# Second product of an MLP: instructions of VectorE, GpSimd and ScalarE's casts tied to the order of the source

## The chip, the cores and the metric

The kernel runs on one core of a Trainium2 chip. A core has TensorE (PE: matmuls, with its weight loads shown apart as PEld), VectorE (DVE), ScalarE (ACT), GpSimd (POOL) and SyncE (SP, which here issues most DMAs). Each engine works through its own queue in the order in which the instructions stand there; engines wait for each other by semaphores. The metric is the time of one execution on the device in microseconds, the median of several runs.

## The reference

A block with two parallel mixers (a long convolution and gated linear attention), then a two-layer MLP. The change concerns only the end:

```python
def _sq_relu_mlp(h, w1, w2):
    return jnp.square(jax.nn.relu(h @ w1)) @ w2
...
        x = x + g2 * _sq_relu_mlp(h2, w_mlp1[l], w_mlp2[l])
...
    return _rms_norm(x, norm_final)
```

Here x has 2048 rows of 1024 and the MLP's inner width is 4096; all is float32. `g2` is a gate of 1024 columns.

## The kernel before

**Precision.** A float32 operand is split into a high part (a cast on ACT, `uh`, `wh`, `bh`) and a low part (a subtraction on DVE or POOL, `ul`, `wl`, `bl`), and a product is made of three matmuls: high by high, high by low, low by high.

**Seven products.** Both products of the MLP use a scheme of Strassen's kind: a 2 x 2 block product with seven multiplications m = 1 to 7 in the order 1, 2, 6, 5, 7, 4, 3 instead of eight. Sums of blocks are formed first (`sum_b`, L1243 and L1245, and the two subtractions L1464 and L1465 for a chunk of the second weights).

**The second product** is the loop over `at` from 0 to 63, called a step here: `t = at % 8` is a pair of row tiles and `g = at // 8` a part of the inner dimension. A step has seven *groups*, one for each m; a group is six matmuls of 128 x 128 by 512 (`full2`, L1640), three for each of two weights (`wh`/`wl` for kb = 0, `bh`/`bl` for kb = 1). Groups 4 and 3 of a step run late, within the next step (`late4`, `late3`), so in time a step runs 1, 2, 4 of the step before, 6, 3 of the step before, 5, 7. Three accumulators in PSUM serve a step; groups 1, 6, 7 and 4 go on in the same one, `x`, and after each group `more` (L1645) adds it to the rows in SBUF, `acc`, on DVE. So the addition after group 1 must be done before group 6 starts, and so on.

After a group, `refill` splits for the step after (for 4 and 3: for the group that is still to run): an operand `ur` into `uh` (L1598, ACT) and `ul` (L1599, POOL; DVE in step 0), and, where the weight changes, `w2_split`: `wh`/`bh` by ACT and `wl`/`bl` by DVE (the helper `split`, L231 and L232, before), with `sum_b` on DVE. `uh` and `ul` of each m have two buffers (odd and even steps), each weight one.

A **chunk** of the second weights is a tile `raw` of 128 x 5 x 512, loaded by SP (L1458), in one of two buffers. `w2_raw` returns six pieces of work: four *gates* (products with `g2b`, L1461, on POOL) and L1464 and L1465 (on DVE). The loop asks for a chunk in every fourth step (`at % 4 == 3`) and puts the six pieces into a list, `prep`, from which `slot()` takes one entry. `slot()` is called after each group's refill, seven times in a step, here numbered 0 to 6. By the source the gates of a chunk asked for in step 7 come in slots 1, 3 and 5 of step 8 and slot 0 of step 9, L1464 in slot 4 and L1465 in slot 6 of step 9, and its splits from step 10 on.

In the last eight steps a finished pair of row tiles is normalised: ACT squares it (L1660), POOL makes the factor (L1664, L279, L280: `ss`, `mrs`), and `finish` (L1669) scales it on DVE and stores it.

**What sets the order.** The source only traces instructions. A scheduler then orders each engine's queue by priority and by when it takes the inputs of an instruction to be ready; so an instruction may stand far ahead of its place in the source. `tc.keep_in_program_order(ins)` records, for one instruction, that it must come behind the instruction traced before it on its engine. It adds an order within the queue and no semaphore. It was used at one place so far, L323.

Of the kernel before, what the change touches and what calls it, by code (L numbers as in the profile page):

```python
# [10 lines left out]
F32 = mybir.dt.float32  # L11
# [3 lines left out]
ALU = mybir.AluOpType  # L15
# [195 lines left out]
def hybrid_block(ctx: ExitStack, tc, a, out, dbg=None):  # L211
    nc = tc.nc
# [5 lines left out]
    dve = nc.vector  # L218
    gps = nc.gpsimd
# [10 lines left out]
    def split(hi, lo, src):  # L230
        nc.scalar.copy(hi, src)  # L231
        dve.tensor_sub(lo, src, hi.bitcast(F32))  # L232

    dr = ctx.enter_context(tc.tile_pool(name="dram", bufs=1, space=DRAM))
    d_s = dr.tile([32, 128, DH], F32, name="d_s")
# [19 lines left out]
    def sb(name, side="left", stack=ctx):  # L255
        return stack.enter_context(tc.tile_pool(name=name, bufs=1, side=side, reuse_waits="tile"))
# [35 lines left out]
    def load_w(src):  # L292

        n = src.shape[-1]
        hi, lo = (wp.tile([P, KD * 264], F32R, tag=t, bufs=2, name=t)[:, 0:KD * n].rearrange("p (k n) -> p k n", k=KD)
                  for t in ("whi", "wlo"))
        for h in range(2):
            raw = wp.tile([P, 4 * 272], F32, tag="raw", bufs=1, name="raw")
            rk = raw[:, 0:4 * n].rearrange("p (k n) -> p k n", k=4)
            ks = slice(4 * h, 4 * h + 4)  # L300
            dma(rk, src[:, ks, :])
            split(hi[:, ks, :], lo[:, ks, :], rk)
        return hi, lo
# [706 lines left out]
    def load_wo(k):  # L1010
        raw = rawp.tile([P, D], F32, tag="raw", bufs=2, name="raw")
        dma(raw[:], a["w_out"][k * P:(k + 1) * P, :])
        split(woh[k // 4][:, k % 4, :], wol[k // 4][:, k % 4, :], raw[:])
# [3 lines left out]
    def load_y(t, a_):  # L1017
        yt = yop.tile([P, 4, P], F32, tag=f"yt{a_}", bufs=2, name="yt")
        dma(yt[:], d_yt[a_ * DH:(a_ + 1) * DH, t * P:(t + 1) * P].rearrange("(k p) t -> p k t", p=P))
        yh = yop.tile([P, 4, P], F32R, tag=f"yh{a_}", bufs=2, name="yh")  # L1020
        yl = yop.tile([P, 4, P], F32R, tag=f"yl{a_}", bufs=2, name="yl")
        split(yh[:], yl[:], yt[:])
        ys[t, a_] = (yh, yl)
# [197 lines left out]
    def raw_tile():  # L1221
        pool = rp[nraw[0] % len(rp)]
        nraw[0] += 1
        return pool.tile([P, 5, 512], F32, tag="raw", bufs=1, name="raw")
# [5 lines left out]
    PLACE = (0, 1, 2, 3, 4, 0, 1)  # L1230
# [9 lines left out]
    def sum_b(r, m, eng):  # L1240

        if m == 1:
            eng.tensor_sub(r[:, 0, :], r[:, 2, :], r[:, 4, :])  # L1243
        elif m == 2:
            eng.tensor_sub(r[:, 1, :], r[:, 1, :], r[:, 0, :])  # L1245

    def part(kp, h, j):
        return bp[kp].tile([P, 512], F32R, tag=f"b{h}{kp}_{j}", bufs=1, name=f"b{h}")
# [120 lines left out]
    g2b = sb("gp", stack=em).tile([P, D], F32, name="g2b")  # L1369
# [85 lines left out]
    def w2_raw(n, engs, eng=dve):  # L1455

        r = w2r[n] = raw_tile()
        dma(r[:, 0:4, :], a["w2"][n])  # L1458

        def gate(q):  # L1460
            engs[q].tensor_mul(r[:, q, :], r[:, q, :], g2b[:, (q // 2) * 512:(q // 2 + 1) * 512])  # L1461

        return [*(lambda q=q: gate(q) for q in range(4)),
                lambda: eng.tensor_sub(r[:, 4, :], r[:, 3, :], r[:, 0, :]),  # L1464
                lambda: eng.tensor_sub(r[:, 3, :], r[:, 2, :], r[:, 3, :])]  # L1465

    def w2_split(n, m):
        r, j, k = w2r[n], PR[m][1], PR[m][0]
        if n % 2:

            hi, lo = (part(0, h, j) for h in "hl")
        else:
            hi, lo = (wm.tile([P, 512], F32R, tag=f"w{h}{k}", bufs=1, name=f"w{h}") for h in "hl")
        split(hi[:], lo[:], r[:, PLACE[j], :])
        sum_b(r, m, dve)
        w2s[m, n % 2] = (hi, lo)

# [2 lines left out]
    for tb in range(2):  # L1480
# [8 lines left out]
        for at in range(1, 16):  # L1489
            n = ns[at]  # L1490
            w, nxt = wops, {}
            x, y = pt(), pt()
            r, rn = rw[n], None
            first = lambda m: w2_split(0, m) if tb and at == 15 else None
            if at < 15:
                rn = rw[ns[at + 1]] = w_raw(ns[at + 1])
            elif tb == 0:
                raws.append(fill_raw(1, 0, gps))
            else:
                for step in w2_raw(0, [gps] * 4):  # L1500
                    step()
# [21 lines left out]
            if at == 15 and tb == 0:  # L1523
                raws.append(fill_raw(1, 1, gps))
            elif at == 15:
                more_w2 = w2_raw(1, [dve] * 4)
# [47 lines left out]
    def row(at, m, kb):  # L1574
        return 2 * ((at + 8 - CHANGE[m, kb]) // 8 % 8) + kb
# [14 lines left out]
    def u_tile(at, h, m):  # L1590
        return uu[(h, m) not in U0 or at % 2].tile([P, 2, P], F32R, tag=f"u{h}{m}{at % 2}", bufs=1, name=f"u{h}")
# [3 lines left out]
    def split_u(at, m):  # L1595
        hi, lo = (first_u.pop((h, m)) if at == 0 and (h, m) in first_u else u_tile(at, h, m) for h in "hl")
        src = uts[at][:, :, ORDER.index(m), :]
        nc.scalar.copy(hi[:], src)  # L1598
        (gps if at else dve).tensor_sub(lo[:], src, hi[:].bitcast(F32))  # L1599
        ops[at, m] = (hi, lo)  # L1600

    load_u(0)
# [10 lines left out]
    def acc(t, i, j):  # L1613
        return acc4[t // 2][:, 2 * (t % 2) + i, j * 512:(j + 1) * 512]
# [3 lines left out]
    for m in (1, 2, 6):  # L1618
        w2_split(1, m)
        split_u(0, m)  # L1620
    for m in (5, 7):
        w2_split(1, m)
# [9 lines left out]
    for m in (5, 7):  # L1632
        split_u(0, m)
# [8 lines left out]

    def more(ps, t, i, j):

        dve.tensor_add(acc(t, i, j), acc(t, i, j), ps[:])  # L1645

    def refill(at, m):

        if at < NU:
            split_u(at, m)  # L1650
            for kb in range(2):
                n = row(at, m, kb)
                if n != row(at - 1, m, kb) if at else m in (4, 3):
                    w2_split(n, m)
# [7 lines left out]
    def scale_of(t, i):  # L1662
        ss = sums.pop((t, i))
        gps.tensor_add(ss[:, 2:3], ss[:, 0:1], ss[:, 1:2])  # L1664
        return rstd_of(mf, ss[:, 2:3], 1, 1.0 / D, "mrs")

    def finish(t, i, j, rs):
        v, tile = acc(t, i, j), 2 * t + i
        dve.scalar_tensor_tensor(v, v, rs[:], nf[:, j * 512:(j + 1) * 512], op0=ALU.mult, op1=ALU.mult)  # L1669
        dma(out[tile * P:(tile + 1) * P, j * 512:(j + 1) * 512], v)  # L1670

    def slot():
# [9 lines left out]
    for at in range(NU):  # L1682
        g, t = divmod(at, 8)
        prep, coming = prep + coming, []
        x, y = pt(), pt()
        full2(x, at, 1, True)
        more(x, t, 0, 0)
        refill(at + 1, 1)
        slot()
        z = pt()  # L1690
        full2(z, at, 2, True)
        more(z, t, 0, 0)
        refill(at + 1, 2)
        slot()
# [3 lines left out]
        slot()  # L1698
        full2(x, at, 6, False)
        more(x, t, 0, 1)  # L1700
        refill(at + 1, 6)
        slot()
# [8 lines left out]
        if at == 0:  # L1711
            coming = w2_raw(row(4, 1, 1), [gps] * 4, gps)
        elif at % 4 == 3 and at < 60:

            q = w2_raw(row(at + 5, 1, at // 4 % 2), [gps] * 4)
            coming = [v for step in q[:4] for v in (None, step)] + [None] * 3 + [q[4], None, q[5]]
        if at == 40:
            nf = mf.tile([P, D], F32, name="nf")
            dma(nf[:], a["norm_final"].partition_broadcast(P))
        if g == 7 and t:  # L1720
            for i, j in ((0, 0), (0, 1), (1, 0), (1, 1)):
                square(t - 1, i, j)
            for i in range(2):
                rs = scale_of(t - 1, i)
                ends.extend(lambda i=i, j=j, rs=rs, t=t: finish(t - 1, i, j, rs) for j in range(2))
# [28 lines left out]
    for i, rs in ((1, r1), (0, r0)):  # L1754
        for j in range(2):
            finish(7, i, j, rs)
# [18 lines left out]
```

## Time and profile before

| | |
|---|---|
| median of 3 runs | 2677.9 us (2675.67 to 2682.8) |
| profiled execution | 2688.92 us, span 2687.1 us |
| mean granted clock of TensorE | 0.959 |
| busy: PE, PEld, DVE, ACT, POOL | 93%, 77%, 60%, 44%, 40% |
| first matmul of the second product, last one | 1969.9 us, 2677.4 us |
| matmuls L1640 in it | 6 x 448 |

The profile shows one execution; its times are in microseconds from the first instruction. Rows of groups give a line of the kernel, the engine, the instruction and what it writes and reads, with buffer numbers left out. Idle time of an engine is put down to what came last of that for which it waited. The clock that TensorE is granted is a share of full speed.

### The profile page before, as it was taken

What the parts mean: (1) busy time and instruction counts of PE and PEld (TensorE: products, weight loads), DVE (VectorE), ACT (ScalarE), POOL (GpSimd) and SP (SyncE); (2) the same over time, 40 slices, a digit from 0 to 9 for tenths busy, and PEclk for the clock granted to TensorE, in tenths of its full rate; (3) what the DMA queues carried; (4) which work ended last, traced back from release to release, by engine and by line L of the source; (5) the groups of instructions that cost most, each with busy time, mean ns of one, the idle gap of its engine ahead of it and who ended that gap; (6) DMA issues with size and microseconds to landing.
All of it is one profiled execution on the core that took longest, in us unless ns stands there. A gap on an engine that the chain in (4) does not pass through costs nothing. (4 is left out here: it accounts for less than half of the span.)

```text
span 2687.1 us, 38017 instructions
## 1 busy us (share of the span) xinstructions
PE 2506.9 (93%) x13320; PEld 2076.7 (77%) x13320; DVE 1612.6 (60%) x2619; ACT 1185.2 (44%) x2273; POOL 1077.9 (40%) x1093
## 2 busy tenths in 40 slices
PE   9799999999998798899989998999978999999987
PEld 5678978897887787788778887888867777777776
DVE  5754366735567677744465557555556656666668
ACT  6464352225225555334455555555543333333334
POOL 2130231214112213142344443544466666666565
PEclk9899999999998798899999999999998999999999
DMA  5425444432548787556544545545483233323333
GB/s 194 140 86 175 123 134 141 140 117 92 174 148 197 200 238 202 185 169 210 162 144 142 165 137 169 169 141 165 135 310 124 99 114 112 114 99 114 112 125 129
DMA packets 304480, 406.09 MB, mean 151 GB/s; under 512 B 25108, under 2 KB 226712, under 8 KB 293920
## 3 DMA queue, kind: packets, MB, share of 16 engines
q1 hardware_dynamic: 301408, 395.27, 47.0%
q10 hardware_dynamic: 2880, 8.39, 0.8%
q8 instruction: 105, 1.72, 0.3%
q14 instruction: 87, 0.71, 0.1%
HBM read 273.49 MB, written 130.09 MB: 150 GB/s over the span
## 5 line engine op out<-in xcount | busy, mean ns | idle before, releaser
L1599 POOL TENSOR_TENSOR ul<-ur,uh 128x256 fp32r<-128x256 f32 x441 | 360.3, 825 | 209.5 <-ACT uh L1598 209.2
L1645 DVE TENSOR_TENSOR acc<-acc,ps 128x512 f32<-128x512 f32 x448 | 304.0, 683 | 156.8 <-PE ps L1640 154.1
L1598 ACT CAST uh<-ur 128x256 fp32r<-128x256 f32 x448 | 179.1, 406 | 410.3 <-PE ps L1640 378.4
L1384 PE MATMUL ps<-bh,wh 128*128 128x512 f32 x896 | 350.3, 393 | 5.0 <-ACT u L1392 2.1
L1384 PE MATMUL ps<-bl,wh 128*128 128x512 f32 x896 | 351.0, 392 | 4.0 <-DVE bl L232 4.0
L1384 PE MATMUL ps<-bh,wl 128*128 128x512 f32 x896 | 350.1, 391 | 4.1 <-DVE wl L232 4.1
L232 DVE TENSOR_TENSOR wl<-raw,wh 128x512 fp32r<-128x512 f32 x276 | 266.4, 977 | 98.0 <-ACT wh L231 95.4
L231 ACT CAST wh<-raw 128x512 fp32r<-128x512 f32 x276 | 170.6, 622 | 203.7 <-PE ps L1384 166.2
L1640 PE MATMUL ps<-wh,uh 128*128 128x512 f32 x448 | 185.1, 413 | 66.4 <-DVE acc L1645 59.2
L1384 PEld LDWEIGHTS ps<-bh,wh 128*128 128x128 f32 x896 | 169.5, 189 | 42.0 <-ACT tt L1350 3.3
L1384 PEld LDWEIGHTS ps<-bl,wh 128*128 128x128 f32 x896 | 169.5, 189 | 40.4 <-DVE bl L232 5.3
L1384 PEld LDWEIGHTS ps<-bh,wl 128*128 128x128 f32 x896 | 169.3, 189 | 40.4 <-DVE wl L232 5.3
L1640 PE MATMUL ps<-bl,uh 128*128 128x512 f32 x448 | 180.2, 402 | 0.0
L1640 PE MATMUL ps<-bh,ul 128*128 128x512 f32 x448 | 180.0, 402 | 0.0
L1640 PE MATMUL ps<-wl,uh 128*128 128x512 f32 x448 | 179.9, 401 | 0.0
L1640 PE MATMUL ps<-bh,uh 128*128 128x512 f32 x448 | 179.9, 401 | 0.0
L1640 PE MATMUL ps<-wh,ul 128*128 128x512 f32 x448 | 179.6, 401 | 0.0
L1640 PEld LDWEIGHTS ps<-wh,uh 128*128 128x128 f32 x448 | 88.6, 198 | 96.4 <-DVE acc L1645 63.4
L226 PE MATMUL ph<-hth,whi 128*128 128x512 f32 x384 | 150.9, 393 | 0.0
L228 PE MATMUL ph<-hth,wlo 128*128 128x512 f32 x384 | 149.6, 390 | 0.0
L227 PE MATMUL ph<-htl,whi 128*128 128x512 f32 x384 | 149.4, 389 | 0.0
L226 PE MATMUL pv<-whi,hth 128*128 128x264 f32 x512 | 146.7, 287 | 2.8 <-ACT whi L231 2.7
(291 smaller groups left out, 5727.4 us busy)
## 6 DMA issues: line engine op xcount, KB each, us to landing
raw<-in_w_dram SPq DMA_DIRECT2D x49, 1024.0 KB, 5.5
ur<-d_m SPq DMA_DIRECT2D x112, 448.0 KB, 3.9
d_m<-c SPq DMA_DIRECT2D x128, 256.0 KB, 2.6
d_m<-s SPq DMA_DIRECT2D x96, 256.0 KB, 3.4
xt<-in_x_dram SPq DMA_DIRECT2D x32, 512.0 KB, 4.8
mwt<-in_wada_dram SPq DMA_DIRECT2D x64, 256.0 KB, 3.0
raw<-in_wi_vg_dram SPq DMA_DIRECT2D x20, 528.0 KB, 4.8
wada<-in_wada_dram SPq DMA_DIRECT2D x16, 512.0 KB, 7.2
```

Source lines behind the costliest of these rows:

```text
L226: mm(ps, lh, rh, start=first, stop=False)
L227: mm(ps, lh, rl, start=False, stop=False)
L228: mm(ps, ll, rh, start=False, stop=last)
L231: nc.scalar.copy(hi, src)
L232: dve.tensor_sub(lo, src, hi.bitcast(F32))
L1384: mm(ps[:], x_[:, sl], y_[j], start=start and i == 0, stop=stop and i == 2, skip_group_check=True)
L1598: nc.scalar.copy(hi[:], src)
L1599: (gps if at else dve).tensor_sub(lo[:], src, hi[:].bitcast(F32))
L1640: mm(ps[:], x_[:, kb, :], y_[:], start=start and kb + i == 0, stop=kb == 1 and i == 2, skip_group_check=True)
L1645: dve.tensor_add(acc(t, i, j), acc(t, i, j), ps[:])
```

## The change

`pin` is the context's `keep_in_program_order`. It is put around the instructions of the second product on DVE and POOL (gates, L1464 and L1465, low parts, the additions after groups, the final scaling) and around the casts of ACT. `w2_split` no longer calls `split` but writes out the same two instructions. The matmuls, the DMAs, ACT's squares, `sum_b` and POOL's factors aren't pinned.

```diff
+    pin = tc.keep_in_program_order
...
         def gate(q):
-            engs[q].tensor_mul(r[:, q, :], r[:, q, :], g2b[:, (q // 2) * 512:(q // 2 + 1) * 512])
+            pin(engs[q].tensor_mul(r[:, q, :], r[:, q, :], g2b[:, (q // 2) * 512:(q // 2 + 1) * 512]))
 
         return [*(lambda q=q: gate(q) for q in range(4)),
-                lambda: eng.tensor_sub(r[:, 4, :], r[:, 3, :], r[:, 0, :]),
-                lambda: eng.tensor_sub(r[:, 3, :], r[:, 2, :], r[:, 3, :])]
+                lambda: pin(eng.tensor_sub(r[:, 4, :], r[:, 3, :], r[:, 0, :])),
+                lambda: pin(eng.tensor_sub(r[:, 3, :], r[:, 2, :], r[:, 3, :]))]
...
-        split(hi[:], lo[:], r[:, PLACE[j], :])
+        pin(nc.scalar.copy(hi[:], r[:, PLACE[j], :]))
+        pin(dve.tensor_sub(lo[:], r[:, PLACE[j], :], hi[:].bitcast(F32)))
         sum_b(r, m, dve)
...
-        nc.scalar.copy(hi[:], src)
-        (gps if at else dve).tensor_sub(lo[:], src, hi[:].bitcast(F32))
+        pin(nc.scalar.copy(hi[:], src))
+        pin((gps if at else dve).tensor_sub(lo[:], src, hi[:].bitcast(F32)))
...
-        dve.tensor_add(acc(t, i, j), acc(t, i, j), ps[:])
+        pin(dve.tensor_add(acc(t, i, j), acc(t, i, j), ps[:]))
...
-        dve.scalar_tensor_tensor(v, v, rs[:], nf[:, j * 512:(j + 1) * 512], op0=ALU.mult, op1=ALU.mult)
+        pin(dve.scalar_tensor_tensor(v, v, rs[:], nf[:, j * 512:(j + 1) * 512], op0=ALU.mult, op1=ALU.mult))
```

The new lines shift the numbers: in the changed kernel the gates are L1464, L1464 and L1465 are L1467 and L1468, L1599 is L1603, L1598 is L1602, L1645 is L1649, and the split of a weight is L1477 and L1478. Three places in the queues follow.

DVE before, around L1464 of the chunk `raw_18264`; the rows of `acc_17801` belong to steps 4 and 5 (`ps_18019` is `x` of step 5 and `ps_18020` its `y`), those of `acc_17990` to step 6:

```order
L1645 TENSOR_TENSOR acc_17801<-acc_17801,ps_18033 128x512
L1645 TENSOR_TENSOR acc_17801<-acc_17801,ps_17922 128x512
L1645 TENSOR_TENSOR acc_17801<-acc_17801,ps_18019 128x512
L1645 TENSOR_TENSOR acc_17801<-acc_17801,ps_17923 128x512
L1464 TENSOR_TENSOR raw_18264<-raw_18264 128x512
L1645 TENSOR_TENSOR acc_17801<-acc_17801,ps_18020 128x512
L1465 TENSOR_TENSOR raw_18264<-raw_18264 128x512
L1645 TENSOR_TENSOR acc_17801<-acc_17801,ps_18019 128x512
L232 TENSOR_TENSOR wl_18120<-raw_17890,wh_18119 128x512
```

DVE of the change, around the same subtraction of the same chunk (`ps_18391` and `ps_18392` are `x` and `y` of step 9, `acc_17609` stands for step 10):

```order
L1649 TENSOR_TENSOR acc_17481<-acc_17481,ps_18391 128x512
L1649 TENSOR_TENSOR acc_17481<-acc_17481,ps_18297 128x512
L1467 TENSOR_TENSOR raw_18264<-raw_18264 128x512
L1649 TENSOR_TENSOR acc_17481<-acc_17481,ps_18392 128x512
L1649 TENSOR_TENSOR acc_17481<-acc_17481,ps_18391 128x512
L1468 TENSOR_TENSOR raw_18264<-raw_18264 128x512
L1649 TENSOR_TENSOR acc_17609<-acc_17609,ps_18477 128x512
L1478 TENSOR_TENSOR bl_18491<-raw_18264,bh_18490 128x512
L1246 TENSOR_TENSOR raw_18264<-raw_18264 128x512
```

The subtraction moved from step 5 to step 9, the place of the source, right ahead of the splits that need it.

POOL before, around the four gates of that chunk; `ur_17992` holds the operands of step 7, `ur_17887` those of step 6 and `ur_18080` those of step 8:

```order
L1599 TENSOR_TENSOR ul_18149<-ur_17887,uh_18148 128x256
L1461 TENSOR_TENSOR raw_18264<-raw_18264,g2b_12328 128x512
L1599 TENSOR_TENSOR ul_18160<-ur_17992,uh_18159 128x256
L1461 TENSOR_TENSOR raw_18264<-raw_18264,g2b_12328 128x512 x3
L1599 TENSOR_TENSOR ul_18175<-ur_17887,uh_18174 128x256
L1599 TENSOR_TENSOR ul_18189<-ur_17992,uh_18188 128x256
```

POOL of the change, around the same four gates (`ur_18178` holds step 9, `ur_18261` step 10):

```order
L1603 TENSOR_TENSOR ul_18318<-ur_18178,uh_18317 128x256
L1464 TENSOR_TENSOR raw_18264<-raw_18264,g2b_12328 128x512
L1603 TENSOR_TENSOR ul_18330<-ur_18080,uh_18329 128x256
L1603 TENSOR_TENSOR ul_18345<-ur_18178,uh_18344 128x256
L1464 TENSOR_TENSOR raw_18264<-raw_18264,g2b_12328 128x512
L1603 TENSOR_TENSOR ul_18357<-ur_18080,uh_18356 128x256
L1603 TENSOR_TENSOR ul_18376<-ur_18178,uh_18375 128x256
L1464 TENSOR_TENSOR raw_18264<-raw_18264,g2b_12328 128x512
L1603 TENSOR_TENSOR ul_18388<-ur_18178,uh_18387 128x256
L1603 TENSOR_TENSOR ul_18401<-ur_18261,uh_18400 128x256
L1464 TENSOR_TENSOR raw_18264<-raw_18264,g2b_12328 128x512
```

The gates moved from the low parts for step 7 to those for steps 9 and 10, about two steps later, and stand one by one between them.

ACT before, at the first change of weights, in step 2 (`raw_17615` is the first chunk of the loop; `ur_17611` holds step 3, `ur_17703` step 4):

```order
L1598 CAST uh_17813<-ur_17611 128x256
L1598 CAST uh_17824<-ur_17611 128x256
L1598 CAST uh_17837<-ur_17703 128x256
L231 CAST bh_17742<-raw_17615 128x512
L1598 CAST uh_17849<-ur_17703 128x256
L231 CAST bh_17759<-raw_17615 128x512
```

ACT of the change, around the same two casts:

```order
L1602 CAST uh_17725<-ur_17514 128x256
L1602 CAST uh_17738<-ur_17611 128x256
L1477 CAST bh_17742<-raw_17615 128x512
L1602 CAST uh_17755<-ur_17611 128x256
L1477 CAST bh_17759<-raw_17615 128x512
```

The weight's first cast stood behind the first operand of step 4 and now stands behind the first operand of step 3.

## The prediction

> **What bounds the kernel now.** I read the share of busy time first, then the waits of the second product (from 1969.9 us on), then one of its stalls on all four engines, and last the windows of that stage. From the page and from the waits between 2000 us and the end (engine and line that waited, what it waited for: us in total, times, longest):
>
> ```profile
> span 2687.1 us, 38017 instructions
> DVE raw L1464 <- POOL raw L1461: 75.0, 15, 9.2
> PEld ps L1640 <- DVE acc L1645: 63.4, 24, 7.2
> PE ps L1640 <- DVE acc L1645: 59.2, 25, 6.8
> POOL raw L1461 <- DMA raw<-in_w_dram: 14.8, 13, 3.6
> ```
>
> TensorE (PE) waits for the additions L1645 on VectorE (DVE), and DVE waits 15 times, 5.0 us each, for GpSimd's (POOL's) gate products L1461. The weight loads (PEld) wait over the same gaps as the matmuls, so the two middle rows aren't added. One of the 15 in the timeline (start, duration, engine, instruction; in brackets the idle time before it and what ended it), DVE, POOL and PE apart:
>
> ```profile
> 2168.19 0.69 DVE L1645 TENSOR_TENSOR acc<-acc,ps 128x512 f32<-128x512 f32 x1 [0.67 <-PE ps L1640]
> 2173.93 1.20 DVE L1464 TENSOR_TENSOR raw<-raw 128x512 f32<-128x512 f32 x1 [5.05 <-POOL raw L1461]
> 2175.05 0.68 DVE L1645 TENSOR_TENSOR acc<-acc,ps 128x512 f32<-128x512 f32 x1
> ...
> 2167.46 1.29 POOL L1461 TENSOR_TENSOR raw<-raw,g2b 128x512 f32<-128x512 f32 x1 [0.94 <-DMA raw<-in_w_dram]
> 2168.71 0.74 POOL L1599 TENSOR_TENSOR ul<-ur,uh 128x256 fp32r<-128x256 f32 x1
> 2169.41 2.55 POOL L1461 TENSOR_TENSOR raw<-raw,g2b 128x512 f32<-128x512 f32 x2
> 2172.60 1.30 POOL L1461 TENSOR_TENSOR raw<-raw,g2b 128x512 f32<-128x512 f32 x1
> ...
> 2173.21 0.39 PE L1640 MATMUL ps<-bh,ul 128*128 128x512 f32 x1
> 2176.98 0.80 PE L1640 MATMUL ps<-wh,uh 128*128 128x512 f32 x1 [3.39 <-DVE acc L1645]
> 2177.58 0.63 PE L1640 MATMUL ps<-wl,uh 128*128 128x512 f32 x1
> 2181.84 0.63 PE L1640 MATMUL ps<-bh,ul 128*128 128x512 f32 x1
> ```
>
> DVE has nothing else to blame: it stands at L1464 from 2168.9 to 2173.9 while POOL multiplies four rows, the first of them held by its load. The additions behind L1464 come late, PE runs dry, and its next matmuls start 0.426 us apart ((2181.84 - 2177.58) / 10 between the eleven in these rows). In a stretch without a stall they start 0.2266 us apart, 20.17 us for 89 intervals:
>
> ```profile
> 2144.65 0.39 PE L1640 MATMUL ps<-bh,ul 128*128 128x512 f32 x1
> ...
> 2164.82 0.39 PE L1640 MATMUL ps<-bl,uh 128*128 128x512 f32 x1
> ```
>
> The windows of the stage, cut at the restarts of PE (us; busy time and count of PE, PEld, DVE, ACT, POOL; granted clock, DMA share, GB/s):
>
> ```profile
> 1969.88:2020.00 50.12, 38.69 (x151) 30.58 (x151) 25.92 (x38) 14.79 (x42) 41.44 (x45) 0.87 0.83 311
> 2019.94:2048.60 28.66, 26.05 (x102) 20.97 (x102) 15.88 (x24) 9.59 (x22) 17.63 (x22) 0.90 0.39 130
> 2048.61:2565.11 516.50, 480.82 (x2016) 392.10 (x2016) 318.72 (x469) 181.12 (x420) 329.78 (x385) 0.95 0.33 110
> 2565.12:2609.50 44.38, 39.88 (x168) 32.54 (x168) 26.50 (x40) 18.05 (x45) 28.72 (x37) 0.96 0.36 121
> 2609.51:2678.00 68.49, 62.16 (x252) 47.45 (x252) 60.86 (x85) 31.63 (x86) 43.85 (x68) 0.98 0.36 128
> ```
>
> At 0.2266 us a matmul these stretches would take 34.2, 23.1, 456.8, 38.1 and 57.1 us. So they lose **15.9, 5.5, 59.7, 6.3 and 11.4 us**, 98.8 together. The third one holds twelve periods of four steps (168 matmuls), each 5.0 us too long.
>
> **What the change moves.** It adds and removes no arithmetic: the same multiplications, casts and subtractions, in another order. In the order before, L1464 of a chunk of weights stood four steps ahead of its place in the source (for the chunk raw_18264 in step 5, not 9), and its gates in one block among the low parts for step 7. Now the gates stand singly between the low parts that steps 8 and 9 issue, the last in slot 0 of step 9, and L1464 in slot 4 of step 9. Between the last gate and L1464 lie four more slots, that is four groups of six matmuls, 4 x 6 x 0.2266 = 5.4 us. POOL needs 1.29 us for the gate, so L1464 finds it done.
>
> *Term 1, the periodic stalls: 5.5 + 59.7 + 6.3 = 71.5 us.* All of it goes if nothing else is late. What is late next, by engine, in one step of 7 groups, 9.52 us:
> DVE: seven additions at 0.60 (their spacing when queued: 2175.05 to 2175.65 below), and where weights are split up to three subtractions and two sums at 0.60, each subtraction behind its cast (0.65):
>
> ```profile
> 2175.65 0.68 DVE L1465 TENSOR_TENSOR raw<-raw 128x512 f32<-128x512 f32 x1
> 2150.49 0.69 DVE L232 TENSOR_TENSOR wl<-raw,wh 128x512 fp32r<-128x512 f32 x1 [0.65 <-ACT wh L231]
> L1645 DVE TENSOR_TENSOR acc<-acc,ps x448: 671/686/690, 1973.2 to 2678.1; 128x512 f32<-128x512 f32 x150
> L1598 ACT CAST uh<-ur x448: 387/407/410, 1969.4 to 2660.7; 128x256 fp32r<-128x256 f32 x150
> L1599 POOL TENSOR_TENSOR ul<-ur,uh x441: 720/737/1266, 1977.0 to 2661.2; 128x256 fp32r<-128x256 f32 x147
> ```
>
> That is 4.2 + 1.8 + 1.2 + 1.95 = 9.15 us in the fullest step, 0.37 under 9.52, and 6.7 in a step with gates (two subtractions). An addition may be late by two groups, 2.7 us, before its accumulator is wanted again. ACT: the cast of a weight waits for the group that still reads the old one, and the casts of operands now stand behind it in the source's place. Their lead over PE shrinks from two steps to one, 9.5 us; after a weight's cast (0.62) and an operand's (0.41) comes the low part (0.74) and at most three gates ahead of it (3.9), 5.7 in all, so 3.8 us are left. If that cover went, PE would wait for low parts (rival B). POOL: 7 x 0.74 + 3 x 1.29 = 9.05 us in the fullest step. SP isn't pinned: the load of a chunk is issued once the chunk before the last in the same buffer has been split (step 4 for the gates of step 8), so the load is hidden, where it held POOL 13 times before. Bounds: all 71.5, or, if both sums of the fullest step take the 1.20 us of L1464 in place of 0.60, DVE has 10.35 us of work there, 0.83 over, and 15 x 0.83 = 12.5 of the 71.5 stay: 59. I take 71.5, since the stretches between the stalls, with the same work on DVE, run without a gap.
>
> *Term 2, the start, 15.9 us lost.* Its two stalls in rows of ACT, DVE, DVE and PE:
>
> ```profile
> 1995.66 0.41 ACT L1598 CAST uh<-ur 128x256 fp32r<-128x256 f32 x1 [3.56 <-DMA ur<-d_m]
> 1996.62 0.90 DVE L232 TENSOR_TENSOR bl<-raw,bh 128x512 fp32r<-128x512 f32 x1 [4.40 <-ACT bh L231]
> 2016.29 1.20 DVE L1464 TENSOR_TENSOR raw<-raw 128x512 f32<-128x512 f32 x1 [9.23 <-POOL raw L1461]
> 2001.80 0.77 PE L1640 MATMUL ps<-wh,uh 128*128 128x512 f32 x1 [3.51 <-DVE acc L1645]
> 2019.94 0.79 PE L1640 MATMUL ps<-wh,uh 128*128 128x512 f32 x1 [6.80 <-DVE acc L1645]
> ```
>
> The first came from an operand's cast of step 4 standing ahead of a weight's cast of step 2 on ACT; that is turned round. The second is an L1464. Against this, SP now issues three loads of 1 MB each (the rows to accumulate on) ahead of the first chunk's load. At the 311 GB/s of this window they take 10 us, and the gates of that chunk stand between low parts that PE wants within two steps. Bounds: 13 (a cold start of 12 slow matmuls stays) and -2 (a wait of 10 us and six gated groups, each 1.29 + 0.74 - 1.36 = 0.67 us too slow). I take 9: the two stalls, 3.5 + 6.8 + 3 of slow matmuls, less 4 for this wait.
>
> *Term 3, the hand-over.* PE's last stall in the first product came from a copy L1392 queued behind two casts on ACT; the copy is now first. But the second product then starts when its operands have landed:
>
> ```profile
> 1958.04 0.50 PE L1384 MATMUL ps<-bh,wh 128*128 128x512 f32 x1 [2.09 <-ACT u L1392]
> 1969.88 0.80 PE L1640 MATMUL ps<-wh,uh 128*128 128x512 f32 x1 [6.11 <-ACT uh L1598]
> ```
>
> 0 to 2 us; I take 1. *Term 4, the last stretch, 11.4 us lost.* Here DVE also scales the results (L1669) and waits for POOL's factors:
>
> ```profile
> DVE acc L1669 <- POOL mrs L280: 8.6, 9, 2.0
> L1669 DVE SCALAR_TENSOR_TENSOR acc<-acc,mrs,nf x32: 737/750/1320, 2607.7 to 2683.3; 128x512 f32<-128x512 f32 x32
> ```
>
> Those waits stay, and DVE is 60.86 us busy of 68.49. The slow restart (2 us) goes, and two subtractions of the last chunk come back into this stretch. Bounds -5 (five steps each 1 us later) to +6; I take 2.
>
> **Sum:** 71.5 + 9 + 1 + 2 = 83.5. The profiled execution took 2688.92 us (its span 2687.1 and 1.8 around it), so 2605 there. The median of the runs shown is 11.0 lower, 2677.9; less 83 that is **2595 us**.
>
> **Rivals.** *A, DVE and POOL in each other's way.* The gates now run while DVE works, where DVE used to stand still. L1464, a subtraction, took 1.20 us beside POOL's work, and L1465, the same form, 0.68. As a mechanism of this kernel: each of four gates holds DVE up for its 1.29 us, 5.2 us a chunk, against 9.52 - 6.7 = 2.8 of slack; 2.4 x 15 = 36 us of the gain go: 2595 + 36 = 2631. Against it: the additions of L1645, most of what DVE does there, took at most 690 ns in all 448, many beside POOL. 0.14. [...] *B, POOL becomes the pace (slower).* If the lead of the low parts is under about 5.7 us when the gates begin, six groups a chunk go at 1.29 + 0.74 = 2.03 us instead of 1.36: 4.0 idle, and 12 x 0.2 = 2.4 of slow matmuls, 6.4 against 5.0 now, so 15 x 1.4 = 21 worse: 2699, with nothing gained elsewhere. For it: POOL has 9.05 us of work in a step of 9.52. Against it: the lead is a full step by the source's order. 0.06. *C, the stalls don't go,* since PE, SP and the squares aren't pinned: 2678; against it stands the order itself. 0.03.
>
> **Numbers.** Forecast 0.77, A 0.14, B 0.06, C 0.03. The range of the forecast goes from the best ends (71.5 + 13 + 2 + 6 = 92.5: 2585) to the worst (59 - 2 + 0 - 5 = 52: 2626), and takes A in: 2585 to 2632. A measurement tells 0.3% (8 us) from no change: faster 0.91, same 0.03, slower 0.06.
>
> **What would show it.** L1464 (now L1467) without an entry over 5 us in the waits; PE's idle time before L1640 under 25 us, the windows of the middle at 168 matmuls in 38.1 us with clock 1.00; POOL's gates without a wait for a load, but for the first chunk. Wrong it would be if PE waits for low parts in every fourth step, or if DVE's subtractions grow beyond 1 us and additions come late.

## The result and the profile after

The changed kernel takes **2615.05 us** (median of 4 runs, 2613.25 to 2622.70) against 2676.78 us for the kernel before (4 runs, 2668.86 to 2682.80): ratio 0.9766, 95% interval 0.9745 to 0.9788. The forecast was 2595, the range 2585 to 2632. Its profiled execution took 2614.02 us (span 2612.2), the one of before 2688.92 (2687.1). In the new numbering the gates are L1464, the two subtractions L1467/L1468, the splits of weights L1477/L1478, the operands' casts and low parts L1602/L1603, the additions L1649, the matmuls L1644, the scaling L1673.

The waits of the changed kernel from 2000 us to the end (us in total, times, longest):

```profile
DVE acc L1673 <- POOL mrs L283: 10.4, 8, 2.5
PEld ps L1644 <- DVE acc L1649: 9.9, 8, 2.9
PE ps L1644 <- DVE acc L1649: 9.4, 8, 2.7
DVE raw L1467 <- POOL raw L1464: 0.8, 1, 0.8
```

DVE's 15 waits for gates, 75.0 us, are one wait of 0.8 us, and PE's 59.2 us behind late additions are 9.4. One chunk in the timeline, POOL's last gate and then DVE around the subtraction:

```profile
2139.35 1.29 POOL L1464 TENSOR_TENSOR raw<-raw,g2b 128x512 f32<-128x512 f32 x1
...
2144.38 0.69 DVE L1649 TENSOR_TENSOR acc<-acc,ps 128x512 f32<-128x512 f32 x1 [0.67 <-PE ps L1644]
2144.98 1.09 DVE L1467 TENSOR_TENSOR raw<-raw 128x512 f32<-128x512 f32 x1
2146.00 0.68 DVE L1649 TENSOR_TENSOR acc<-acc,ps 128x512 f32<-128x512 f32 x1
```

The last gate begins 5.6 us ahead of the subtraction; nothing stands still. For the rest I cut the second product, in every trace, at PE's first matmul of step 4 and of step 57, so that the same work is compared: steps 0 to 3, 4 to 56 and 57 to 63 (168, 2226 and 294 matmuls, which take 38.1, 504.5 and 66.6 us at the prediction's 20.17 / 89 us each). The windows of before, and of after (us; busy time and count of PE, PEld, DVE, ACT, POOL; granted clock, DMA share, GB/s):

```profile
1969.88:2026.78 56.90, 45.47 (x168) 35.91 (x169) 29.68 (x43) 16.18 (x45) 43.57 (x47) 0.84 0.80 300
2026.78:2595.32 568.54, 530.23 (x2227) 432.52 (x2226) 351.41 (x516) 200.70 (x466) 363.11 (x423) 0.95 0.33 110
2595.32:2677.75 82.43, 71.84 (x295) 55.15 (x293) 66.50 (x93) 38.30 (x104) 54.70 (x82) 0.98 0.36 130
```

```profile
1961.74:2016.34 54.60, 46.92 (x169) 35.90 (x170) 36.91 (x50) 18.55 (x48) 32.78 (x36) 0.86 0.80 296
2016.34:2520.89 504.55, 504.55 (x2227) 417.93 (x2226) 365.75 (x516) 175.59 (x468) 366.68 (x427) 1.00 0.38 124
2520.89:2602.96 82.07, 72.68 (x295) 56.32 (x293) 67.28 (x94) 37.90 (x107) 64.36 (x90) 0.96 0.40 138
```

Lost against PE's pace: before 18.8, 64.0 and 15.8 us, after **16.5, 0.1 and 15.4**. Of the second product's gain, 66.6 us, 63.9 lie in the middle. Its two ends, from which the prediction expected 11 us, gave 2.7.

At the start POOL is now the engine that waits: SP (its DMA issues) and POOL in the timeline of after:

```profile
1971.56 1.75 SPq L1615 DMA_DIRECT2D acc<-d_x  x3
...
1976.06 1.06 SPq L1461 DMA_DIRECT2D raw<-in_w_dram  x2
...
1987.80 1.26 POOL L1464 TENSOR_TENSOR raw<-raw,g2b 128x512 f32<-128x512 f32 x1 [15.30 <-DMA raw<-in_w_dram]
1989.02 0.72 POOL L1603 TENSOR_TENSOR ul<-ur,uh 128x256 fp32r<-128x256 f32 x1
```

POOL stands for 15.30 us before the first chunk's first gate, whose load went out behind three of 1 MB, and every low part behind it waits too. Near the end it is DVE, with the scaling in the source's order (POOL, DVE and PE):

```profile
2571.38 1.31 POOL L1464 TENSOR_TENSOR raw<-raw,g2b 128x512 f32<-128x512 f32 x1
2572.63 3.30 POOL L1603 TENSOR_TENSOR ul<-ur,uh 128x256 fp32r<-128x256 f32 x4
...
2576.44 0.55 POOL L283 TENSOR_TENSOR mrs<-mrs,mhalf 128x1 f32<-128x1 f32 x1
...
2577.03 0.75 DVE L1673 SCALAR_TENSOR_TENSOR acc<-acc,mrs,nf 128x512 f32<-128x512 f32 x1 [2.50 <-POOL mrs L283]
...
2578.52 0.76 PE L1644 MATMUL ps<-wh,uh 128*128 128x512 f32 x1 [2.71 <-DVE acc L1649]
```

The factor comes after a gate and four low parts, DVE waits 2.50 us for it, the additions behind the scaling come late, and PE stands for 2.71 us.

### The profile page after: what moved, and what is told of

It reads as the page before. It is cut to its first block, busy times and chain, and to the rows that moved or that the text cites. A ratio compares the mean times of both kernels' runs of the same rounds, so it can differ in the third digit from the quotient of the medians.

```text
span 2612.2 us, 37835 instructions
## 1 busy us (share of the span) xinstructions
PE 2475.5 (95%) x13320; PEld 2058.4 (79%) x13320; DVE 1631.5 (62%) x2619; ACT 1158.3 (44%) x2273; POOL 1081.4 (41%) x1093
## 4 chain that ended last, share of the span: by engine, by line
PE 46%; DVE 4%; DMA 3%; POOL 2%; issue 2%; ACT 1%; SPq 0%; POOLq 0%; DVEq 0%; ACTq 0%
PE ps L1644 21%; PE ps L1387 20%; PE po L228 2%; PE po L227 2%; PE po L226 2%; DVE bl L232 1%; POOL ul L1603 1%; DMA raw<-in_w_dram 1%; DVE wl L232 1%; DMA raw<-d_h 1%; DMA raw<-in_w_out_dram 0%; DMA ur<-d_m 0%; DMA d_h<-tt 0%; POOL raw L1464 0%; PE ps L1349 0%
## 5 line engine op out<-in xcount | busy, mean ns | idle before, releaser
L1603 POOL TENSOR_TENSOR ul<-ur,uh 128x256 fp32r<-128x256 f32 x441 | 362.7, 850 | 144.4 <-ACT uh L1602 144.4
L1649 DVE TENSOR_TENSOR acc<-acc,ps 128x512 f32<-128x512 f32 x448 | 303.3, 684 | 150.6 <-PE ps L1644 147.1
L232 DVE TENSOR_TENSOR wl<-raw,wh 128x512 fp32r<-128x512 f32 x217 | 223.8, 1046 | 83.6 <-ACT wh L231 81.4
L231 ACT CAST wh<-raw 128x512 fp32r<-128x512 f32 x217 | 134.1, 622 | 171.4 <-PE ps L1387 161.4
L1644 PE MATMUL ps<-wh,uh 128*128 128x512 f32 x448 | 177.6, 397 | 18.5 <-DVE acc L1649 10.1
L1644 PE MATMUL ps<-wh,ul 128*128 128x512 f32 x448 | 177.0, 395 | 4.5 <-POOL ul L1603 3.4
L1602 ACT CAST uh<-ur 128x256 fp32r<-128x256 f32 x448 | 151.8, 401 | 59.9 <-DMA ur<-d_m 46.9
L1644 PE MATMUL ps<-bl,uh 128*128 128x512 f32 x448 | 176.4, 394 | 0.0
L1644 PE MATMUL ps<-bh,uh 128*128 128x512 f32 x448 | 176.4, 394 | 0.0
L1644 PE MATMUL ps<-wl,uh 128*128 128x512 f32 x448 | 176.2, 393 | 0.0
L1644 PE MATMUL ps<-bh,ul 128*128 128x512 f32 x448 | 176.1, 393 | 0.0
L227 PE MATMUL pv<-wlo,hth 128*128 128x264 f32 x512 | 145.7, 285 | 0.8 <-DVE wlo L232 0.8
```

The source lines that it names most:

```text
L227: mm(ps, lh, rl, start=False, stop=False)
L1602: pin(nc.scalar.copy(hi[:], src))
L1603: pin((gps if at else dve).tensor_sub(lo[:], src, hi[:].bitcast(F32)))
L1644: mm(ps[:], x_[:, kb, :], y_[:], start=start and kb + i == 0, stop=kb == 1 and i == 2, skip_group_check=True)
L1649: pin(dve.tensor_add(acc(t, i, j), acc(t, i, j), ps[:]))
```

## Experiments

Theory P: the stalls came from where the chunk's subtraction stood on DVE, and its place alone takes them away. Rival O: the order of casts and additions did it. Rival G: the gates' place did. Later came theories on the two ends: L (the late load), M (the scaling ahead of its factors), and their rivals K, N and D. All were run beside the kernel before, 4 to 10 times each. The kernel before itself gave medians of 2686.1, 2684.2 and 2680.5 us in the three groups, so ratios are compared, and losses in the traces.

| run | median us | ratio, 95% interval | lost in steps 0–3 | 4–56 | 57–63 |
|---|---|---|---|---|---|
| no_raw | 2689.18 | 1.0012, 0.9989–1.0035 | 21.6 | 63.5 | 16.3 |
| raw_only | 2617.61 | 0.9744, 0.9702–0.9786 | 9.9 | 0.1 | 12.9 |
| subs_only | 2621.02 | 0.9765, 0.9717–0.9812 | 10.4 | 4.8 | 16.2 |
| gates_only | 2632.17 | 0.9800, 0.9761–0.9840 | 15.4 | 13.8 | 14.3 |
| early_load | 2623.19 | 0.9779, 0.9764–0.9794 | 13.7 | 0.7 | 15.4 |
| start_shift | 2618.75 | 0.9776, 0.9758–0.9794 | 14.4 | 0.9 | 15.3 |
| late_scaling | 2613.22 | 0.9740, 0.9727–0.9754 | 18.9 | 0.1 | 9.3 |
| no_gate_pin | 2629.81 | 0.9803, 0.9790–0.9817 | 19.2 | 4.8 | 14.5 |
| after_again | 2620.12 | 0.9766, 0.9733–0.9798 | 18.8 | 0.1 | 15.6 |
| both_ends | 2609.34 | 0.9725, 0.9694–0.9756 | 10.3 | 0.1 | 9.9 |
| raw_and_scaling | 2607.10 | 0.9722, 0.9689–0.9755 | 9.4 | 0.1 | 9.4 |
| raw_scaling_early | 2602.88 | 0.9700, 0.9669–0.9732 | 3.3 | 0.1 | 10.8 |

### Which of the instructions kept in order does it

Four kernels keep only some of the instructions in the source's order (`pin(...)`). no_raw frees the gates and the two subtractions and keeps the rest:

```diff
-            pin(engs[q].tensor_mul(r[:, q, :], r[:, q, :], g2b[:, (q // 2) * 512:(q // 2 + 1) * 512]))
+            engs[q].tensor_mul(r[:, q, :], r[:, q, :], g2b[:, (q // 2) * 512:(q // 2 + 1) * 512])
...
-                lambda: pin(eng.tensor_sub(r[:, 4, :], r[:, 3, :], r[:, 0, :])),
-                lambda: pin(eng.tensor_sub(r[:, 3, :], r[:, 2, :], r[:, 3, :]))]
+                lambda: eng.tensor_sub(r[:, 4, :], r[:, 3, :], r[:, 0, :]),
+                lambda: eng.tensor_sub(r[:, 3, :], r[:, 2, :], r[:, 3, :])]
```

> All of the change but the gates and the two subtractions of a chunk (L1464, L1467, L1468). Theory P: the stalls are back, 15 waits of about 5 us of DVE for POOL, 2665 to 2685 us. Rival O: most of the gain stays, 2615 to 2640 us.

raw_only is the reverse, gates and subtractions alone:

```diff
-        pin(nc.scalar.copy(hi[:], r[:, PLACE[j], :]))
-        pin(dve.tensor_sub(lo[:], r[:, PLACE[j], :], hi[:].bitcast(F32)))
+        nc.scalar.copy(hi[:], r[:, PLACE[j], :])
+        dve.tensor_sub(lo[:], r[:, PLACE[j], :], hi[:].bitcast(F32))
...
-        pin(dve.tensor_add(acc(t, i, j), acc(t, i, j), ps[:]))
+        dve.tensor_add(acc(t, i, j), acc(t, i, j), ps[:])
```

(so too in `split_u` and `finish`.)

> Only the gates L1464 and the two subtractions L1467/L1468 of a chunk stay in the source's order; casts, splits, additions and the scaling go where they went before. Theory P (the place of the chunk's subtraction on DVE made the stalls): the 71.5 us of the periodic stalls stay gone, the first chunk's load is issued behind one 1 MB load and not three, so about 2610 us (2600 to 2620). Rival O (the order of the casts and additions made the gain): only a few us of gain are left, 2660 to 2677 us.

subs_only is raw_only without the line on the gates, gates_only is raw_only without the two on the subtractions.

> Only the two subtractions L1467/L1468 keep the source's order; the gates stand on POOL in one block four steps early, as before. Theory P: the subtraction finds its gates long done, no wait of DVE for POOL over 1 us in the middle, about 2610 us (2600 to 2620). Rival G (the gates have to stand singly between the low parts, or low parts come late behind the block): about 12 x 3 us of the gain go, 2645 us or more. Rival O: 2660 to 2677 us.

> Only the gates L1464 keep the source's order, so they end in step 9 of a period, while the subtraction L1467 stands on DVE a step earlier than in the changed kernel, behind the first group of step 8. Theory P: DVE waits longer than before, 5 to 9 us a chunk, so 2677 to 2740 us. Rival G: the gain stays for the most part, about 2620 us.

The waits of no_raw from 1950 us on:

```profile
DVE raw L1467 <- POOL raw L1464: 82.0, 15, 6.6
```

The window of its middle steps:

```profile
2030.67:2598.63 567.96, 524.17 (x2228) 428.42 (x2226) 356.70 (x516) 175.65 (x468) 358.06 (x427) 0.97 0.34 112
```

The middle steps of subs_only:

```profile
2007.89:2517.14 509.25, 507.34 (x2227) 416.80 (x2226) 364.00 (x516) 200.35 (x466) 385.26 (x428) 1.00 0.37 126
```

Rival O falls: with everything kept but these three lines the 15 waits are back and the time is that of before; with them alone the ratio is that of the whole change. Two instructions a chunk, the subtractions, bring 59.2 of the 64.0 us (64.0 - 4.8), although the gates stand in a block four steps early again. Theory P holds. The gates' place isn't without effect, though: gates_only, with the gates alone kept in order, brings 50.2 us (64.0 - 13.8). The scheduler then moved the free subtraction as well, to right behind the last gate (below). So by these runs what counts is how long after the last gate DVE comes to the subtraction, and either of the two edits lengthens that time. By their times raw_only came within the 2600 to 2620 us expected; subs_only ended 1 us above its range and no_raw 4 us above, in a group where the kernel before took 2686.1 us.

gates_only missed its expectation: 5 to 9 us a chunk were expected, and it lost 13.8 us over 14 chunks. One of them on DVE, POOL and PE:

```profile
2140.34 1.29 POOL L1464 TENSOR_TENSOR raw<-raw,g2b 128x512 f32<-128x512 f32 x1
...
2141.67 1.22 DVE L1467 TENSOR_TENSOR raw<-raw 128x512 f32<-128x512 f32 x1 [2.46 <-POOL raw L1464]
...
2146.03 0.47 PE L1644 MATMUL ps<-wh,uh 128*128 128x512 f32 x1 [0.75 <-DVE acc L1649]
```

DVE comes only 2.46 us too early, and of these PE sees 0.75, with no slow matmuls behind. A wait of 5.05 us cost PE 5.0 before (3.39 of idle time and slow matmuls), one of 2.46 cost about 1 (13.8 / 14): by an estimate from these two (5.05 less 3.39, 2.46 less 1) the first 1.5 us or so didn't reach PE, and behind the long wait the slow matmuls came on top.

### The start

early_load keeps the loads in order too and puts the first chunk's ahead of the others; start_shift has its gates two slots later besides:

```diff
-        dma(r[:, 0:4, :], a["w2"][n])
+        pin(dma(r[:, 0:4, :], a["w2"][n]))
...
-        if g == 0 and t < 6:
-            load_acc(t + 2)
+        if at == 0:
+            coming = w2_raw(row(4, 1, 1), [gps] * 4, gps)
         if at + 3 < NU:
             load_u(at + 3)
-        if at == 0:
-            coming = w2_raw(row(4, 1, 1), [gps] * 4, gps)
+        if g == 0 and t < 6:
+            load_acc(t + 2)
```

(so too the loads in `load_u` and `load_acc`, and that of `nf`; start_shift: `coming = [None] * 2 + w2_raw(...)`.)

> The changed kernel, with the loads of the second product kept in the source's order too, and the first chunk's load put ahead of the three 1 MB loads of the rows to accumulate on. In the changed kernel steps 0 to 3 lose 16.5 us (52.6 to 54.6 us for 168 matmuls that take 38.1), steps 4 to 57 none, steps 58 to 63 15.1. Theory L (the first gate, kept in order, waits for a load that came late): the gate's wait of 15.3 us falls to under 8, the first four steps lose about 10 us, about 6 us less in all, 2609 us. Rival K (the gates between the low parts pace the start whenever the load lands): 15 us or more are still lost there, 2615 us.

> As the run with the early load, and the first chunk's gates asked for two slots later, so that six more low parts stand ahead of the first of them. Theory L: POOL waits for the load by under 6 us with more low parts done, the first four steps lose 7 to 9 us (what is left is the restart at the hand-over and the third step), 8 us less than the changed kernel, 2607 us. Rival K: no better than the early load alone.

Step 0 and steps 1 to 3 of after, and the same two of early_load (at PE's pace steps 1 to 3 take 28.6 us):

```profile
1961.74:1978.20 16.46, 14.63 (x43) 10.46 (x44) 15.79 (x22) 10.03 (x26) 7.43 (x8) 0.73 1.05 381
1978.20:2016.34 38.14, 32.30 (x128) 25.44 (x127) 21.12 (x28) 8.52 (x22) 25.34 (x28) 0.91 0.69 260
```

```profile
1971.13:1992.02 20.89, 14.14 (x43) 9.57 (x43) 19.68 (x23) 10.20 (x26) 12.01 (x10) 0.77 0.63 231
1992.02:2022.88 30.86, 28.83 (x127) 23.57 (x126) 20.14 (x28) 8.53 (x22) 25.47 (x28) 1.00 0.72 264
```

Steps 1 to 3 lose 2.3 us in place of 9.6. The gate still waits 10.9 us (15.3 in after), not under 8, but counted from the first matmul of step 1 it runs after 2.2 us (1994.21) in place of 9.6 (1987.80). But step 0 loses 11.4 in place of 6.9, and the ratio is no better. The loss has a place: kept in order, chunk 1's load also moved, behind the stores of the first product. In the timeline it went out at 1943.60 in after, 18 us ahead of the first matmul of step 0, and here at 1960.29, 11 us ahead:

```profile
1958.96 1.24 SPq L1427 DMA_DIRECT2D d_m<-s  x2
1960.29 0.60 SPq L1461 DMA_DIRECT2D raw<-in_w_dram  x1
```

So the edit did more than was meant, and the next ones keep loads in order from step 0 on only. start_shift shows the same (12.7 us in step 0). Both missed their expected times, 2609 and 2607 us.

### The last steps

late_scaling asks for the scaling three slots later; no_gate_pin is the changed kernel with the line on the gates freed:

```diff
+            ends.extend([None] * 3)
             for i in range(2):
                 rs = scale_of(t - 1, i)
```

> The changed kernel, with the scaling of the results L1673 asked for three slots later, so that POOL's factors are there when DVE comes to it. Theory M (DVE, now in the source's order, stands before the factors; 10.4 us of waits in 8 places): the waits of DVE for POOL's factors fall under 4 us, steps 58 to 63 lose about 11 us in place of 15.1, 4 us less, 2611 us. Rival D (DVE is simply full there, 10 us of work or more a step): 14 to 16 us are still lost, 2615 us.

> The changed kernel, with the gates L1464 alone free again: they stand on POOL in one block, four steps early, but for the first chunk's, whose place is unchanged. Theory N (the last chunk's gates between the low parts hold back POOL's factors and so the scaling): steps 58 to 63 lose 12 us in place of 15.1. Rival D: 14 to 16. Both: no loss in the middle steps, the first four steps as in the changed kernel, 16 us; 2611 to 2615 us.

The waits of late_scaling from 1950 us on:

```profile
DVE acc L1673 <- POOL mrs L283: 2.6, 3, 1.4
```

The window of its last steps:

```profile
2523.93:2599.86 75.93, 69.56 (x295) 54.18 (x293) 69.17 (x92) 37.91 (x107) 65.96 (x90) 1.00 0.42 146
```

Theory M holds: 9.3 us lost in place of 15.4, with the same work: DVE is busy 69.17 us of 75.93, where it was 67.28 of 82.07, so rival D falls with it. Theory N falls: with the last chunk's gates early the last steps still lose 14.5. By its ratio no_gate_pin is about 0.4% slower than the changed kernel, where 2611 to 2615 us were expected. Against its expectation it loses the same 4.8 us in the middle as subs_only. A chunk of subs_only on DVE and on POOL shows what stands there:

```profile
2061.16 1.74 DVE L1467 TENSOR_TENSOR raw<-raw 128x512 f32<-128x512 f32 x1
2062.82 1.47 DVE L1649 TENSOR_TENSOR acc<-acc,ps 128x512 f32<-128x512 f32 x2
2064.21 1.10 DVE L1468 TENSOR_TENSOR raw<-raw 128x512 f32<-128x512 f32 x1
...
2068.13 1.78 DVE L1478 TENSOR_TENSOR bl<-raw,bh 128x512 fp32r<-128x512 f32 x1
...
2061.06 1.30 POOL L1464 TENSOR_TENSOR raw<-raw,g2b 128x512 f32<-128x512 f32 x1 [2.18 <-DMA raw<-in_w_dram]
2062.31 1.20 POOL L1603 TENSOR_TENSOR ul<-ur,uh 128x256 fp32r<-128x256 f32 x1
2063.46 3.00 POOL L1464 TENSOR_TENSOR raw<-raw,g2b 128x512 f32<-128x512 f32 x2
```

Gates four steps early run beside the subtractions and splits of the chunk before. This chunk is one of the worst: over the middle steps of subs_only L1467 and L1468 take 0.89 and 1.20 us (medians), 1.09 and 0.69 in after, and a split L1478 up to 1.79, 1.07 in after. The loss lies in steps 6, 10, 14 and so on, up to 0.9 us in each; there DVE has most to do, 8.57 us of work on average, 8.32 in after. That the overlap makes the 4.8 us fits the rows; it wasn't tried by itself.

### Both ends together

The last group has the changed kernel again, and three that join the mends. In both_ends and raw_scaling_early the loads are kept in order from step 0 on (`if n > 1: pin(d)`, and so in the others), with the first chunk's first:

> The changed kernel itself, beside the three that follow: 0.977 of the kernel before, the same losses in its trace (16.5 us in steps 0 to 3, none to step 57, 15.1 from there).

> The changed kernel with both mends: the first chunk's load ahead of the others and its gates two slots later, now with the loads kept in order from step 0 on only, so that the loads at the hand-over stay where the changed kernel has them; and the scaling three slots later. Theory L and M together: the first four steps lose 9 us (7 of them in the first), the last six 9: 13 us less than the changed kernel, 0.972 of before. If the loss of 11 to 13 us that the two runs with early loads showed in the first step was not the load of chunk 1 behind the stores, it shows here again: then 5 us less only.

> Gates, the two subtractions and the scaling kept in the source's order, the scaling three slots later, all else free as before. The first four steps as in the run with gates and subtractions alone (10 us), the last six 9 us: about 12 us less than the changed kernel, 0.972 of before. If the casts and additions have to keep their order for the scaling to fit between them, the last six lose 12 us or more.

> As the run before, with the first chunk's load ahead of the others and the loads kept in order from step 0 on. Theory L: the load of operands that the third step waits for goes out earlier, the first four steps lose 6 to 8 us, 0.971 of before. If that load waits for the buffer only, as free gates leave it, no better than the run before.

after_again repeats the ratio; its start lost 18.8 us and not 16.5, so 2 us there are no difference. both_ends got 10.3 and 9.9 us, near the 9 and 9 expected; its step 0 lost 8.2 us, where the two runs with all loads kept in order had lost 11.4 and 12.7 and the changed kernel 6.9; so most of that excess came from the loads at the hand-over, of which chunk 1's is the one seen to move. raw_and_scaling came as expected. raw_scaling_early did better than expected. The windows of its step 0 and of its steps 1 to 3:

```profile
1959.40:1972.13 12.73, 12.29 (x43) 9.15 (x43) 10.89 (x13) 5.79 (x18) 12.24 (x14) 0.83 1.06 379
1972.13:2000.80 28.67, 28.67 (x128) 23.58 (x127) 19.36 (x28) 10.88 (x27) 25.73 (x29) 1.00 0.80 299
```

POOL at its first gates, in the timeline (here L1605 are the low parts, L1466 the gates):

```profile
1966.17 7.75 POOL L1605 TENSOR_TENSOR ul<-ur,uh 128x256 fp32r<-128x256 f32 x10 [0.41 <-ACT uh L1604]
1973.86 5.07 POOL L1466 TENSOR_TENSOR raw<-raw,g2b 128x512 f32<-128x512 f32 x4
```

The gate begins without a wait, 14.5 us after the first matmul of step 0 (26.1 in after), and steps 1 to 3 lose 0.1 us in place of 9.6. In both_ends, with the gates one by one between the low parts as in the changed kernel, steps 1 to 3 lose 2.1 us (10.3 less the 8.2 of step 0), with this gate:

```profile
1986.40 1.29 POOL L1466 TENSOR_TENSOR raw<-raw,g2b 128x512 f32<-128x512 f32 x1 [8.23 <-DMA raw<-in_w_dram]
```

It runs 2.0 us after the first matmul of step 1 (1984.44). So it is L and not K: the gates between the low parts cost little once the load comes that early. This version, **2602.88 us (ratio 0.9700)** against 2620.12 of the changed kernel in the same group, is the fastest by its median; its interval overlaps those of raw_and_scaling and both_ends. It keeps in order only the gates, the two subtractions, the scaling and, from step 0 on, the loads.

## Why the prediction was right, and where not

*What bounds the kernel, and term 1 (71.5 us).* Right, in mechanism and size: the stretch that lost 71.5 by the prediction's cuts (matmuls 151 to 2436) loses 0.1 in after, up to 2530 us, and two pinned subtractions do nearly all of it. The lower bound's worry (both sums at 1.20 us in the fullest step) came in part, since one of them, L1248, has a median of 1.11 us there, and cost nothing. Of the signs named, L1467 has no entry over 0.8 us from 2000 us on, PE's idle time before L1644 is 23.0 us in all, POOL's gates wait for one load, the first chunk's, and the middle runs at clock 1.00. (A small slip in its windows: the first holds one matmul of the next stretch and the last ends 0.25 us behind PE, so they lost 16.1 and 11.1 us, not 15.9 and 11.4; these are used below.)

*Term 2, the start (9 us).* Wrong, and the step is "less 4 for this wait". The load's delay was seen and priced at 10 us, of which 4 were to reach PE. POOL stood 15.30 us, not 10, and held back every low part behind the gate: PE waited 2.83 and 0.61 us for low parts (1989.80 and 1992.18). At 2002.62 it waited 2.41 us more for a cast of ACT; ACT had stood 6.21 us behind a sum of the late chunk, and then for operands whose load went out at 1996.00 only. By the prediction's cuts 16.5 us are lost where 16.1 were: of the two stalls the second went, the first stayed at the same matmul (2.41 us, 3.51 before) behind another wait, and others came that cost as much as was gained. The lower bound of -2 held it. That the order of the loads is the cause is shown by early_load and both_ends, with 2.3 and 2.1 us lost in steps 1 to 3 in place of 9.6; these edits move the operands' loads too, and the first chunk's wasn't moved alone. The 6.9 us of step 0 (3.8 before) were not foreseen. PE in step 0 of after:

```profile
1969.07 0.50 PE L1644 MATMUL ps<-wh,ul 128*128 128x512 f32 x1 [1.09 <-DVE ul L1603]
1970.55 0.68 PE L1644 MATMUL ps<-wh,uh 128*128 128x512 f32 x1 [0.74 <-DVE acc L1649]
```

The first of these waits, for a low part that DVE makes, stands before the 15th matmul in all six runs that lose 6.9 us or more in step 0 (1.09 to 3.49 us), and in none of the eight that lose 3.2 to 4.3. Among the eight are no_raw and no_gate_pin, which keep casts and additions in order as well, so it takes the gates kept in order besides. Two low parts on DVE took 1.82 us in after (1968.08), beside low parts on POOL, and one took 0.42 with nothing on POOL beside it (1965.99); what makes them late stays open.

*Term 3, the hand-over (1 us).* Right: PE's idle time there is 0.68 and 5.97 us, where it was 2.09 and 6.11, 1.6 us less.

```profile
1950.03 0.50 PE L1387 MATMUL ps<-bh,wh 128*128 128x512 f32 x1 [0.68 <-ACT u L1395]
1961.74 0.80 PE L1644 MATMUL ps<-wh,uh 128*128 128x512 f32 x1 [5.97 <-ACT uh L1602]
```

*Term 4, the last stretch (2 us).* Wrong in sign by the prediction's cuts (15.4 us lost where 11.1 were), and within its bound of -5. The step is "those waits stay": the waits for the factors did grow only from 8.6 to 10.4 us, but in the source's order the additions queue behind them, and the slow restart that was to go came back behind another stall. late_scaling shows 6 us of it. With equal steps (57 to 63) the loss is the same as before, 15.4 and 15.8: 4 us of "last stretch" stood before in the stall counted under term 1.

*From the profiled execution to the median (11 us).* The terms gave 83.5 us; their parts measured 71.4, -0.5, 1.6 and -4.3, together 68.2. The spans differ by 74.9, so 6.7 us of the profiled difference lie outside the second product, nearly all ahead of it, where the change moves nothing; the medians differ by 61.7. The profile of before was 12.1 us over its final median, that of after 1.0 under its own, and how much of the 12.1 lay in the second product can't be told from one execution. Of the 20 us between 2595 and 2615, 15.3 are the terms, in effect 2 and 4. The other 5 are 12.0, since after's profile lay 1.0 under its median where 11.0 above was assumed, less the 6.7, which were luck. The forecast's own worst end, 2626, held the two misses; rival A, for which the range went to 2632, wasn't needed for it.

*The rivals.* A, DVE and POOL in each other's way: L1467 took longer beside low parts of POOL (a median of 1.09 us, up to 1.55) than with nothing of POOL beside it (0.69 at 2525.78), while L1468, the same form, took 0.68 to 0.69 beside low parts too. That was not over the slack, and the middle loses 0.1 us. So half of a sign of being wrong appeared, subtractions beyond 1 us, and the other half, late additions, didn't: none of the 448 additions of after, whose second operand is in PSUM, took more than 0.69 us, though 378 of them ran beside POOL. B, POOL as the pace: not in the middle; in steps 1 to 3, with a late load, PE waited 3.4 us for POOL's low parts. C's outcome, with the stalls in place, is what no_raw shows.

## What to carry to other kernels

When an engine that runs its queue in order waits, look for the one instruction at its head whose input comes late, and move or hold that one alone: two of the nine lines held in order here brought 59.2 of the 64.0 us of the middle steps. There can be more than one such place to hold (the gates' line alone brought 50.2, as the subtraction moved with it). Holding an instruction in order also holds all that is queued behind it, so before doing it see that its load goes out early (POOL's 15.30 us) and that its input is not the end of another engine's queue (DVE's 2.50 us before the scaling). A short wait cost little here (2.46 us cost 1), and behind a longer one a slow restart of PE was often paid as well (5.05 us cost 5.0).

## What the runs showed of the hardware

Behind some idle gaps of about 2 us and more PE ran slowly for a while (0.426 us a matmul, 0.2266 at its pace), and behind others it didn't. In after, and then in late_scaling, PE in the timeline:

```profile
2539.23 0.50 PE L1644 MATMUL ps<-wh,uh 128*128 128x512 f32 x1 [2.47 <-DVE acc L1649]
...
2540.74 0.62 PE L1644 MATMUL ps<-bh,uh 128*128 128x512 f32 x1
2541.16 0.63 PE L1644 MATMUL ps<-bl,uh 128*128 128x512 f32 x1
```

```profile
2585.95 0.50 PE L1644 MATMUL ps<-wh,uh 128*128 128x512 f32 x1 [2.17 <-DVE acc L1649]
2586.29 0.40 PE L1644 MATMUL ps<-wl,uh 128*128 128x512 f32 x1
...
2587.00 0.40 PE L1644 MATMUL ps<-bl,uh 128*128 128x512 f32 x1
```

After 2.47 us of idle time six matmuls ran at full pace, and only then eight at 0.426 us, 3.4 us together; after 2.17 us none was slow. Counted by the idle time before a matmul in all fourteen traces, from step 4 on: of 94 gaps of 0.4 to 2 us three, of 1.79 to 1.95 us, were followed by slow matmuls, of 40 gaps of 2 to 3.6 us 22 were, and all 7 longer ones, by 5 to 12 of them (in before and after, two of the fourteen, none of 11, 13 of 14 and both of 2). Two gaps close together did it with less: in step 0 of after eight slow matmuls ran behind 1.09 and 0.74 us (1969.07 and 1970.55 above). What decides it the traces don't show.
